# A hybrid attention and retention block: second half's retention gate, queries and keys as seven block products, h sums kept in HBM

## The chip, the core and the metric

The kernel is one program on one NeuronCore of a Trainium2 chip. The metric is the device time of one execution in microseconds; the kernel before takes 517.6 us (median of three runs, 517.25 to 517.76). PE is the matmul engine, DVE and ACT the two vector engines, POOL the general one, SP the engine that only issues transfers. [...] The profile is that of one execution.

## What is computed

One decoder block over x of 512 tokens by 1024 channels, float32. Cut to what matters:

```python
h = rms_norm(x, norm_pre)
(q_n, k_c, v_c, k_s, v_s, k_w, v_w, g_n, z_n,
 q_r, k_r, v_r, z_r, m_a, m_b) = jnp.split(h @ w_in, split_points(), axis=-1)
o_a = nsa(rope(q_n), rope(k_c), v_c, rope(k_s), v_s, rope(k_w), v_w, g_n + b)   # three masked softmaxes, gated
y_a = (o_a * silu(z_n)) @ w_nsa_o
o_b = retention(rope(q_r), rope(k_r) * 128 ** -0.5, v_r)     # 4 heads, chunks of 128, a state R per head, group norm
y_b = (o_b * silu(z_r)) @ w_ret_o
merged = sigmoid(m_a) * y_a + sigmoid(m_b) * y_b
y = x + rms_norm(merged @ w_out, norm_post)
```

w_in is 1024 by 6936. With 512 tokens every selected block is in reach and the window covers all of the past, so the selected and the sliding branch are two full causal attentions.

## The kernel before

**Number form.** Every large product takes float32 operands split in two parts of a rounded format, a high part (whi, hTh) and a low part (wlo, hTl), and uses three matmuls per tile: high by high, low by high, high by low. ACT rounds the high part (L204), DVE subtracts for the low part (`sub_split`, L216). The normed input h lies transposed in hTh and hTl, 8 tiles of 128 channels by 512 tokens; the norm's factor per token is applied to the products (`rs`).

**Weight stream.** All weights lie in HBM in the order of use. SP loads them in pieces of 512 KB into four buffers `raw` (`load_next`, L385 and L388); `splitter` and `split_lo` make whi and wlo of them, each piece in two halves, up to nine halves ahead of PE. A load waits for the low part that frees its buffer.

**Order of work.** One Python pass writes all queues: coroutines ask for buffers and times, class `Order` keeps a clock per engine with assumed costs, and issues whichever is due (`run`; `MARGINS` and `SLACK` set how late a piece counts as due). Nothing of the order is decided on the chip: each engine follows its queue, and waits where an operand is late. The blocks of PE's main line are, after the attention projections and the compression products, those of PLAN: Z (attention's gate), MA (merge gate a), ZR, QK and VR (retention gate, queries with keys, values of heads 0 and 1), ZR, QK and VR of heads 2 and 3, MB, the output products NO and RO, and the second halves MA, NO, MB, RO, last the product with w_out. Attention's steps (`att_head`, `att_block`, `att_cmp`, `att_sum`) are laid between the matmuls of Z to VR, retention's (`ret`) between those of VR and later.

**Seven products.** The second halves of MA and MB and the w_out product do a 2 by 2 block product with seven instead of eight block products (Strassen's scheme in Winograd's form). It needs sums of weight quarters and sums of h quarters. The weight sums are made in HBM: POOL issues copies and accumulating transfers (`weight_sums` L365 and L367, for MA and MB; `out_sums` L351 and L353, for w_out). Those of MA and MB are let go in portions as attention's tiles finish (`CAPS`, released by a one-element copy `mark`, L983, which holds POOL's queue until that tile is there). Those of w_out are issued three or one at a time behind retention's steps: in `ret`, POOL raises the variance to the power -0.5 (`rv`, L216) for the group norm, and `OSUMS` transfers follow. The h sums for MA and MB are made late (`h_sums`, `h_sum`): xT is loaded again, ACT scales it, DVE adds and subtracts, and both split.

**Second half of retention.** ZR and QK of heads 2 and 3 are two blocks, for each of four token tiles 8 x 3 matmuls of 512 columns (`nat`): 192 in all. `tail_zr` makes the gate, `tail_qk` rotates queries and keys straight from the accumulator.

**Attention's small products.** `tail_q` rotates a tile of queries, splits it, and transposes the rounded pair of each head (eight groups of four transposes). `att_cmp` doubles the probabilities of the compressed branch and transposes two blocks for each of two groups.

Of the kernel before, what the change touches and what calls it, by code (L numbers as in the profile page):

```python
# [28 lines left out]
PLAN = (("Z", 0), ("MA", 0), ("ZR", 0), ("QK", 0), ("VR", 0), ("ZR", 1), ("QK", 1), ("VR", 1),  # L29
# [6 lines left out]
MARGINS = {"att_sum": 400.0, "tail_m": 250.0}  # L36
SOON = 2
ISSUE = 8.0
SLACK = 900.0
WAKE = 7  # L40
HOLD_C = 1800.0
EARLY = 1300.0
HOLD = 800.0
OSUMS = (3, 3, 3, 3, 1, 1, 1, 1)
CAPS = (0, 4, 8, 11, 14, 16, 16, 16, 16)
DVE_BIAS = 400
# [97 lines left out]
def block_kernel(ctx: ExitStack, tc, x, xT, x0s, ws, small, w2s, norm_post, rope_r, dmask, out):  # L144
# [5 lines left out]
    cp.tile([P, 48], FT, name="pad")  # L150
# [108 lines left out]
    identp = ep.tile([P, P], FT, name="identp")  # L259
# [31 lines left out]
    xt = [at(o, D) for o in (16, 20, 32, 0)]  # L291
# [4 lines left out]
    KD2 = Ring([at(8 + i, 256) for i in range(2)])  # L296
    NAT = Ring([bp.tile([P, 512], FT, name=f"nat{i}") for i in range(4)])
    PR = Ring([at(8 + 2 * i, 512) for i in range(8)])
    SMC = Ring([(at(27, 256).rearrange("p (h c) -> p h c", h=8), at(24, 512).rearrange("p (h c) -> p h c", h=8))])
# [6 lines left out]
    sgw = [bp.tile([P, 2048], FT, name="sg"), at(30, 2048)]  # L306
# [3 lines left out]
    XH = Ring([at(o, 512) for o in (38, 40)])  # L310
# [12 lines left out]
    sums, osums, oissued, atts = [], [], [], [0]  # L323
    mark = sp.tile([P, 1], FT, name="mark")
    for pieces in stream_shape():
        if pieces == "seven":
            b11, b12, b21, b22 = (ws[off + i * P * 1024:off + (i + 1) * P * 1024].rearrange("(p n) -> p n", p=P)
                                  for i in range(4))
            t1, t2, t3, t4 = (dp.tile([P, 1040], FT, name=f"t{len(sums)}{i}")[:, 0:1024] for i in range(4))
            sums.append(((t1, b11), (t3, b12), (t2, b11), (t4, b21), (t1, b12), (t3, b22), (t2, t3), (t4, t2)))  # L330
# [3 lines left out]
        if pieces == "out":  # L334
            b11, b12, b21, b22 = ([ws[off + i * P * 1024:off + (i + 1) * P * 1024].rearrange("(p n) -> p n", p=P)
                                   for i in range(2 * q, 2 * q + 2)] for q in range(4))
            t1, t2, t3, t4 = ([dp.tile([P, 1040], FT, name=f"o{i}{j}")[:, 0:1024] for j in range(2)] for i in range(4))
            for a, b in ((t1, b11), (t3, b12), (t2, b11), (t4, b21), (t1, b12), (t3, b22), (t2, t3), (t4, t2)):
                osums.extend(zip(a, b))
            loads.extend((a, [1024]) for q in (b11, t3, t2, t4, t1, b21, b22) for a in q)  # L340
            continue
        loads.append((off, pieces))
        off += P * sum(pieces)

    def out_sums(n):

        for _ in range(n):
            i = len(oissued)
            o, a = osums[i]
            if i < 8:  # L350
                G.dma_start(o, a)  # L351
            else:
                G.dma_start(o, a, accum_op=OP.add)  # L353
            od.op("pool", 900.0)
            oissued.append(i)

    def weight_sums():

        for n in range(8):
            for i, block in enumerate(sums):  # L360
                while n * len(sums) + i >= CAPS[atts[0]]:
                    yield lambda: n * len(sums) + i < CAPS[atts[0]]
                o, a = block[n]
                if n < 4:
                    G.dma_start(o, a)  # L365
                else:
                    G.dma_start(o, a, accum_op=OP.add)  # L367
                od.op("pool", 900.0)
# [4 lines left out]
    def in_ring(p):  # L373

        return min(p, KD) + max(p - 2 * KD, 0)
# [20 lines left out]

    def used_up(r):

        done.append(r)
# [3 lines left out]
    def splitter():  # L403
        for i, (_, pieces) in enumerate(loads):
            n = sum(pieces)
            for k in range(2):
                p = 2 * i + k
                late = p - 2 * len(loads) + 8
                own = KD <= p < 2 * KD or late >= 0
                if late >= 0:  # L410
                    yield od.need("gb")
                yield lambda: own or in_ring(p) < in_ring(len(done)) + NW
# [4 lines left out]
                r = max(raws[i][1], done[-1] if done and not own else 0.0)  # L417
# [3 lines left out]
                if late >= 0:  # L421
                    hi, lo = at(4 * late, 512, FR), at(4 * late + 2, 512, FR)
                elif own:
# [5 lines left out]
                if p:  # L429
# [8 lines left out]
    def split_lo(p, hi, lo, src, vh, vl, r):  # L438
        yield lambda: rank(p)() == 0 or od.eng["dve"] <= od.now + SLACK
        yield r  # L440
        r = sub_split(vl, src, vh, r)
# [7 lines left out]
    def rank(p):  # L449

        return lambda: 0 if p <= wanted[0] + SOON else 4

# [50 lines left out]
    x0 = ep.tile([P, KD + 256], FT, name="x0")  # L503
# [12 lines left out]
    def load_x(t):  # L516
        r = max(hready[0:2]) if t == NT - 1 else 0.0
        DMA.dma_start(xt[t], x[t * P:(t + 1) * P, :])
        xr_[t] = od.dma(P * D * 4, r)
# [12 lines left out]
    def h_low(k, e):  # L532
# [3 lines left out]
        od.flags.add(f"h{k}")  # L536

# [87 lines left out]
    def tail_a(t, ps, e, ring):  # L625
# [12 lines left out]
        yield e + HOLD  # L638
# [35 lines left out]

    def tail_z(j, ps, e):
# [9 lines left out]
        NAT.put(th, e)  # L685
        od.flags.add(f"Z{j}")
# [95 lines left out]
    def tail_q(t, ps, e):  # L782
# [6 lines left out]
        qs = qT[t].rearrange("p h (s c) -> p h s c", s=2)  # L789
        qv = qn.rearrange("p (h c) -> p h c", h=8)  # L790
# [4 lines left out]
        for g in range(2):  # L795
            pt = yield from PT.get()
            yield e + PE_LAG
            for j in range(4):
                ep = tr(pt.bitcast(FR)[:, j * P:(j + 1) * P],
                        qs[:, g * 4 + j].rearrange("p a b -> p (a b)"), identr, e)  # L800
            yield ep, "act"
            ep = act(qT[t][:, g * 4:g * 4 + 4, :], pt.rearrange("p (h c) -> p h c", h=4), r=ep)
            PT.put(pt, ep)
# [15 lines left out]
    def att_cmp(t):  # L819
# [5 lines left out]
        for h in range(8):  # L825
# [20 lines left out]
        e = tt(s3.rearrange("p h (r c) -> p h r c", r=2), sm.unsqueeze(2).broadcast_to([P, 8, 2, 32]),  # L846
               zc.unsqueeze(2).unsqueeze(3).broadcast_to([P, 8, 2, 32]), OP.mult, e)
        for g in range(2):
# [9 lines left out]
            pv = pc.rearrange("p (i j c) -> p i j c", i=2, j=2)  # L858
            tv = pt[:, 0:2 * P].rearrange("p (i c) -> p i c", i=2)
            yield ep, "act"  # L860
            for j in range(2):
                eh = act(pv[0:64, :, j, :], tv[j * 64:j * 64 + 64], r=ep)
            yield eh, "dve"
            for j in range(2):
                ep = tt(pv[32:64, :, j, :], tv[j * 64 + 32:j * 64 + 64], f(pv[32:64, :, j, :]), OP.subtract, eh)
# [5 lines left out]
    def att_head(t, g, brs, j, slot, stat):  # L871
# [6 lines left out]
        e = mm(sv, q, kB[:, b0:b0 + nb, g, 0:L], False, True)  # L878
        yield e, "dve"
# [12 lines left out]
        slot["pv"], slot["z"] = pv, e  # L892

# [73 lines left out]
    def att_sum(t, g, po):  # L967
# [10 lines left out]
        yield e, "pool"  # L978
# [4 lines left out]
        G.tensor_copy(mark[m], gv[:, 0, 0:1])  # L983
        od.op("pool", 70.0, e)
        atts[0] += 1
# [35 lines left out]
    def tail_qk(hp, t, ps, e):  # L1021
        yield od.need("q0", "q1", "q2", "q3", "cmp0", "cmp1", *([f"ret{hp - 1}{t}"] if hp else []))
# [12 lines left out]
        ACC.put(ps, e)  # L1035
        if 4 * hp + t + 1 < 8:
            load_rtab(4 * hp + t + 1, e)
        yield e, "pool"
# [15 lines left out]
        od.flags.add(f"qk{hp}{t}")  # L1054

    rr, dmr, qend = [0.0], [], [0.0] * NT

    def ret(hp, t, ps, e):
# [24 lines left out]
        if t < NT - 1:  # L1083
            knh, knl = yield from KNHL.get()
            ek = act(knh, kf[t])
            yield ek, "pool"
# [47 lines left out]
        if hp or t >= 2:  # L1134
            VR[1].put((vh, vl), e)
        yield eo, "dve"
# [9 lines left out]
        out_sums(OSUMS[4 * hp + t])  # L1146
# [70 lines left out]
    shr = [0.0] * 4  # L1217

    def h_sums():

        yield od.need(*[f"qk1{t}" for t in range(NT)], *ATT)
        for k in range(4):
            if k == 1:
                yield od.need("ga", *RETA)
                sum_tiles()
                od.flags.add("sums")
            xs = []
            for i in range(2):
                if k:
                    xs.append((yield from XH.get()))  # L1230
                else:
                    xs.append((maskp, at(28, 512))[i])
                DMA.dma_start(xs[i], xT[(4 * i + k) * P:(4 * i + k + 1) * P, :])
                e = od.dma(P * 2048, 0.0) + 1500.0
            od.spawn(h_sum(k, xs, e), 5)

    def h_sum(k, xs, r):
        yield od.need("sums")
        yield r, "act"
        for i in range(2):  # L1240
            e = act(xs[i], xs[i], r=r, scale=gp[:, 4 * i + k:4 * i + k + 1])
        a = yield from NAT.get()
        b = yield from NAT.get()
        yield e, "dve"
        tmp = (a[:, 0:256], a[:, 256:512], b[:, 0:256], b[:, 256:512])
        a11, a21, a12, a22 = (xs[i // 2][:, i % 2 * 256:(i % 2 + 1) * 256] for i in range(4))
        e2 = tt(tmp[2], a22, a21, OP.subtract, e)
        e0 = stt(tmp[0], tmp[2], -1.0, a11, OP.mult, OP.subtract, e2)
        yield e0, "dve"
        e1 = tt(tmp[1], a11, a21, OP.subtract, e)  # L1250
# [553 lines left out]
```

## Time and profile before

| what | value |
|---|---|
| median of three runs | 517.6 us |
| the profiled execution | 517.32 us, span 515.4 us |
| granted PE clock | 0.999 |
| PE, weight loads, DVE, ACT, POOL busy | 506.2, 433.7, 419.2, 303.8, 40.1 us |
| HBM read, written | 77.79 MB, 18.87 MB |
| transfers issued by SP (q1), by POOL (q0) | 62.99 MB, 16.78 MB |

The span goes from the first instruction to the last; the execution has some 1.9 us around it. A row of a timeline gives start, duration, engine, line, operation, out<-in and count; a row of a table of stretches gives the stretch, its length, busy time (and instructions) of PE, weight loads, DVE, ACT and POOL, the granted clock, the DMA engines' mean busy share and GB/s. In a row of DMA queues stand packets, MB and the share of 16 engines' time.

### The profile page before, as it was taken

The page shows a single profiled execution, that of the slowest core. Times are in us where ns is not written, and L with a number is a line of the kernel's source. Part 1 is how long each engine was busy: PE and PEld are TensorE (multiplying, and loading weights), DVE is VectorE, ACT ScalarE, POOL GpSimd, SP SyncE. Part 2 cuts the span into 40 slices and gives each one's busy share as a digit, 9 for nine tenths or more (in the row PEclk, how much of TensorE's full clock was granted, in tenths as well). Part 3 has the DMA queues.
Part 4 walks back from the last instruction along what each step waited for, and adds up shares of the span by engine and source line. Part 5 has one row for each costly group of instructions (what it writes and reads, how often), then busy time and mean ns, then how long its engine had stood idle before and what let it go on. Part 6 is the DMA issues. An engine that isn't in the chain of part 4 may idle for free.

```text
span 515.4 us, 7802 instructions
## 1 busy us (share of the span) xinstructions
PE 506.2 (98%) x2714; PEld 433.7 (84%) x2714; DVE 419.2 (81%) x990; ACT 303.8 (59%) x659; POOL 40.1 (8%) x76
## 2 busy tenths in 40 slices
PE   9999999999999999999999999999999999999995
PEld 7898788888888888888888888888888999988884
DVE  5798799988979798887776666787997876889796
ACT  6673599677677989662544443462664434437642
POOL 3000000000211011100303100202000000000010
PEclk9999999999999999999999999999999999999999
DMA  8942026501764637634565944272842745453814
GB/s 314 373 165 83 22 82 212 197 1 41 239 210 104 184 52 171 167 95 151 169 239 128 257 117 132 42 245 42 250 159 79 229 143 162 157 174 122 318 53 160
DMA packets 25624, 80.39 MB, mean 156 GB/s; under 512 B 2801, under 2 KB 4081, under 8 KB 25585
## 3 DMA queue, kind: packets, MB, share of 16 engines
q1 hardware_dynamic: 20832, 62.99, 35.8%
q0 software_dynamic: 4608, 16.78, 14.1%
q8 instruction: 21, 0.34, 0.3%
q14 instruction: 19, 0.15, 0.1%
q10 hardware_dynamic: 144, 0.14, 0.1%
HBM read 77.79 MB, written 18.87 MB: 188 GB/s over the span
## 4 chain that ended last, share of the span: by engine, by line
PE 88%; DVE 5%; DMA 4%; ACT 1%; issue 1%; SPq 0%; DVEq 0%; POOLq 0%; POOL 0%; ACTq 0%
PE bank L237 75%; PE bank L1555 7%; PE bank L241 6%; DMA arena_l<-in_x_dram 2%; DVE arena_r L216 1%; DMA arena_l<-in_xT_dram 1%; DMA raw<-in_stream_dram 1%; DVE wlo L216 1%; DVE arena_f L216 1%; ACT arena_r L204 1%; DVE arena_l L885 0%; DVE nat L216 0%; DVE arena_l L216 0%; SPq L513 0%; SPq L385 0%
## 5 line engine op out<-in xcount | busy, mean ns | idle before, releaser
L204 ACT ACTIVATE whi<-raw 128x512 fp32r<-128x512 f32 x160 | 96.7, 627 | 44.4 <-PE bank L237 34.7
L216 DVE TENSOR_TENSOR wlo<-raw,whi 128x512 fp32r<-128x512 f32 x176 | 115.4, 684 | 8.6 <-ACT whi L204 8.0
L237 PE MATMUL bank<-whi,hTh 128*128 128x512 f32 x256 | 100.0, 406 | 0.2 <-ACT hTh L204 0.2
L237 PE MATMUL bank<-whi,hTl 128*128 128x512 f32 x256 | 96.2, 391 | 0.0
L237 PE MATMUL bank<-wlo,hTh 128*128 128x512 f32 x256 | 96.1, 391 | 0.0
L237 PE MATMUL bank<-arena_r 128*128 128x256 f32 (+2 forms) x328 | 69.5, 335 | 0.0
L237 PE MATMUL bank<-arena_r,whi 128*128 128x512 f32 (+1 forms) x208 | 63.6, 381 | 0.0
L216 DVE TENSOR_TENSOR arena_r<-bank,arena_r 128x512 fp32r<-128x512 f32 (+2 forms) x80 | 48.1, 606 | 18.1 <-ACT arena_r L204 17.5
L204 ACT ACTIVATE arena_r<-bank 128x512 fp32r<-128x512 f32 (+2 forms) x88 | 46.6, 536 | 23.8 <-PE bank L241 21.0
L204 ACT ACTIVATE arena_l<-arena_l,stat 128x384 f32<-128x384 f32 (+3 forms) x102 | 54.0, 557 | 7.4 <-DVE stat L885 4.0
L237 PEld LDWEIGHTS bank<-whi,hTl 128*128 128x128 f32 x256 | 48.0, 188 | 10.6
L237 PEld LDWEIGHTS bank<-whi,hTh 128*128 128x128 f32 x256 | 48.6, 190 | 9.0 <-ACT hTh L204 0.5
L237 PEld LDWEIGHTS bank<-arena_r 128*128 128x128 f32 x328 | 50.8, 190 | 5.7
L237 PEld LDWEIGHTS bank<-wlo,hTh 128*128 128x128 f32 x256 | 48.2, 188 | 8.4
L237 PE MATMUL bank<-hTh,whi 128*128 128x512 f32 (+1 forms) x144 | 52.6, 365 | 0.0
L237 PE MATMUL bank<-hTh,wlo 128*128 128x512 f32 (+1 forms) x144 | 51.2, 355 | 0.0
L237 PE MATMUL bank<-hTl,whi 128*128 128x512 f32 (+1 forms) x144 | 51.1, 355 | 0.0
L237 PEld LDWEIGHTS bank<-arena_r,whi 128*128 128x128 f32 x208 | 39.0, 188 | 7.4
L237 PE MATMUL bank<-arena_r,wlo 128*128 128x512 f32 x96 | 37.4, 389 | 0.0
L241 PE MATMUL bank<-ident,arena_l 128*128 128x128 f32 x216 | 32.3, 272 | 0.0
L241 PEld LDWEIGHTS bank<-ident,arena_l 128*128 128x128 f32 x216 | 26.8, 140 | 6.5
L237 PEld LDWEIGHTS bank<-hTh,wlo 128*128 128x128 f32 x144 | 27.2, 189 | 4.0
(211 smaller groups left out, 817.1 us busy)
## 6 DMA issues: line engine op xcount, KB each, us to landing
raw<-in_stream_dram SPq DMA_DIRECT2D x75, 512.0 KB, 4.3
t<-in_stream_dram POOLq DMA_DIRECT2D x12, 512.0 KB, 5.1
o<-in_stream_dram POOLq DMA_DIRECT2D x12, 512.0 KB, 5.3
raw<-t SPq DMA_DIRECT2D x8, 512.0 KB, 3.4
raw<-o SPq DMA_DIRECT2D x8, 512.0 KB, 3.9
arena_f<-in_rope_r_dram SPq DMA_DIRECT2D x8, 256.0 KB, 2.7
t<-t POOLq DMA_DIRECT2D x4, 512.0 KB, 5.9
o<-o POOLq DMA_DIRECT2D x4, 512.0 KB, 5.3
```

The lines of the kernel that those rows point to most:

```text
L204: S.activation(o, i, func, **kw)
L216: (V if e == "dve" else G).tensor_tensor(o, a, b, op=op)
L237: T.matmul(ps, a, b, start=start, stop=stop)
L241: T.transpose(ps, a, idn)
L1555: T.matmul(ps[m], a, b, start=n in first and s + i == 0, stop=n in last and s + i == 5, skip_group_check=True)
```

## The change

Four parts.

1. **PAIR.** The blocks ZR 1 and QK 1 become one block `pair`: the 512 tokens by 1024 columns (queries, keys, gate) over 1024 channels as seven products of 24 matmuls. A product goes into two accumulator banks, X and Q in turn, and a bank is used again when its content was kept (ACT copies it to `Z` or `U`) or joined (DVE adds the kept part). The gate and the rotation then read from SBUF.
2. **h sums in HBM.** Early, ACT scales xT by plus or minus the norm's weight (`signed`), SP stores the quarters (22 stores of 128 KB), and POOL adds three tables in HBM (`hsums`). The sums are then loaded in the weight stream, once for PAIR and once for MA and MB, and split like weights into `SB`. `h_sums` and `h_sum` go.
3. **All sums at once.** `add_sums(27)` issues every copy and accumulation in one row behind one `mark`, which waits for the first tile of Z: PAIR's, the h sums, MA's and MB's together in transfers of 1 MB, then w_out's. `OSUMS` is zero. The room for descriptors of POOL's transfers is four times as large.
4. **Smaller ones.** `tail_q` transposes first (four groups of four) and splits after, `att_cmp` transposes one block per group, the loads and order constants are set anew.

```diff
-PLAN = (("Z", 0), ("MA", 0), ("ZR", 0), ("QK", 0), ("VR", 0), ("ZR", 1), ("QK", 1), ("VR", 1),
+PLAN = (("Z", 0), ("MA", 0), ("ZR", 0), ("QK", 0), ("VR", 0), ("PAIR", 1), ("VR", 1),
...
-OSUMS = (3, 3, 3, 3, 1, 1, 1, 1)
-CAPS = (0, 4, 8, 11, 14, 16, 16, 16, 16)
-DVE_BIAS = 400
+OSUMS = (0, 0, 0, 0, 0, 0, 0, 0)
+FIRST = 27
+DVE_BIAS = 500
...
+    hsums = [(two(s02), s21.unsqueeze(1).broadcast_to([P, 2, 1024])), (s1, stab[0]), (s3, s1)]
...
+    sums = ((t1, b11), (t3, b12), (t2, b11), (t4, b21), (t1, b12), (t3, b22), (t2, t3), (t4, t2))
+    seq = [(o, a, i >= 4) for s in (psums, sums, osums) for i, (o, a) in enumerate(s)]
+    for i, h in zip((4, 7, 9), hsums):
+        seq[i:i] = [(*h, True)]
...
+    def add_sums(n):
...
+            o, a, add = seq[issued[0]]
+            if add:
+                G.dma_start(o, a, accum_op=OP.add)
             else:
                 G.dma_start(o, a)
+            od.op("pool", 7000.0 if add else 1000.0)
...
     def weight_sums():
...
+        yield od.need("hq", "Z0")
+        G.tensor_copy(mark, szn[:, 0, 0:1])
+        od.op("pool", 70.0, zready[0])
+        add_sums(FIRST)
...
+    def signed(k, e):
...
+        for i in range(2):
+            e = act(o[i], v[i], r=e, scale=(gp, ngp)[(i + k // 4 + 1) % 2][:, k:k + 1])
+        yield e + 200.0
+        c = slice(k % 4 * 256, k % 4 * 256 + 256)
+        for t, i in ((stab[2], 1), (stab[1], 1), (s21, 0)) if k < 4 else ((stab[0], 0), (stab[3], 1)):
+            DMA.dma_start(t[:, c], o[i])
...
-        e = act(qs[:, :, 0, :], qv, r=e)
-        yield e, "dve"
-        e = sub_split(qs[:, :, 1, :], qv, qs[:, :, 0, :], e)
+        pt = yield from PT.get()
+        yield e + PE_LAG
+        for i in range(4):
+            ep = tr(pt[:, i * P:(i + 1) * P], qn[:, i * P:(i + 1) * P], ident, e)
...
-            for i in range(2):
-                ep = tr(pt[:, i * P:(i + 1) * P],
-                        s3[:, g * 4 + 2 * i:g * 4 + 2 * i + 2, :].rearrange("p h c -> p (h c)"), ident, e)
+            ep = tr(pt[:, 0:P], s3[:, g * 4:g * 4 + 4, :].rearrange("p h c -> p (h c)"), ident, e)
...
+    def pair():
+        blk = Block(36, 512)
+        X, Q = [(yield from ACC.get())], []
+        U, Z = (maskp, at(22, 512)), zt[1]
...
+        plan = ((X, quarter(0, 0), None), (Q, summed(2), 4), (X, summed(1), 10), (Q, quarter(1, 1), None),
+                (X, summed(0), 20), (Q, quarter(0, 1), None), (X, summed(3), 30))
...
+            if n >= 2:
+                lst = {2: p1, 3: p7, 4: u1}.get(n)
+                if lst is not None:
+                    yield lambda: len(lst) == 2
+                    r = max(lst)
+                else:
+                    yield lambda: all((n - 2, m) in fr for m in range(2))
+                    r = max(fr[n - 2, m] for m in range(2))
+                yield r + PE_LAG
...
+                        for j, (a, b) in enumerate(((lh, wh), (ll, wh), (lh, wl))):
+                            T.matmul(ps[m], a, b, start=n in first and s + j == 0, stop=n in last and s + j == 5,
+                                     skip_group_check=True)
...
-    nc = bacc.Bacc("TRN2", target_bir_lowering=False, num_devices=1, dynamic_dma_scratch_size=512)
+    nc = bacc.Bacc("TRN2", target_bir_lowering=False, num_devices=1, dynamic_dma_scratch_size=2048)
```

How the order moves, at two places. POOL's queue from the last sums of MA and MB to retention's first groups, before (t are the sums of MA and MB, o those of w_out, L351 copies and L353 and L367 add):

```order
L367 DMA t_119<-t_117 128x1024
L367 DMA t_123<-t_121 128x1024
L983 COPY mark<-arena_l 64x1 x3
L216 TENSOR_TENSOR rv<-rv,nhalf 128x2
L351 DMA o_124<-in_stream_dram 128x1024
L351 DMA o_125<-in_stream_dram 128x1024
L351 DMA o_128<-in_stream_dram 128x1024
L216 TENSOR_TENSOR rv<-rv,nhalf 128x2
```

The same place now (out are the sums of w_out, L376 copies and L374 adds):

```order
L376 DMA out_126<-in_stream_dram 128x2x1024
L376 DMA out_128<-in_stream_dram 128x2x1024
L376 DMA out_127<-in_stream_dram 128x2x1024
L376 DMA out_129<-in_stream_dram 128x2x1024
L374 DMA out_126<-in_stream_dram 128x2x1024
L374 DMA out_128<-in_stream_dram 128x2x1024
L374 DMA out_127<-out_128 128x2048
L374 DMA out_129<-out_127 128x2048
L216 TENSOR_TENSOR rv<-rv,nhalf 128x2 x8
```

All sums stand ahead of the first of the eight rv, where w_out's stood between them. DVE's queue in the second half, before, where retention's gate and rotation follow each other (wlo are low parts of weights, L229 on nat rotates from the accumulator):

```order
L216 TENSOR_TENSOR wlo<-raw,whi 128x512 x4
L216 TENSOR_TENSOR arena_r<-bank_91,arena_r 128x4x128
L216 TENSOR_TENSOR wlo<-raw,whi 128x512 x3
L229 SCALAR_TENSOR_TENSOR arena_l<-nat_113,arena_l 128x512
L229 SCALAR_TENSOR_TENSOR nat_111<-bank_87,rs_135,arena_f 128x4x64 x2
L229 SCALAR_TENSOR_TENSOR nat_110<-bank_87,rs_135,arena_f 128x4x64 x2
L216 TENSOR_TENSOR nat_111<-nat_111,nat_110 128x4x64 x2
```

And now, in PAIR (maskp<-bank and arena_l<-bank of 512 columns are joins, arena_r<-raw low parts of h sums):

```order
L216 TENSOR_TENSOR maskp<-bank_93,maskp 128x512
L216 TENSOR_TENSOR arena_l<-bank_92,arena_l 128x512
L216 TENSOR_TENSOR wlo<-raw,whi 128x512 x2
L216 TENSOR_TENSOR arena_r<-raw,arena_r 128x512
L216 TENSOR_TENSOR arena_r<-arena_l,arena_r 128x256
L216 TENSOR_TENSOR arena_r<-raw,arena_r 128x512
L216 TENSOR_TENSOR arena_l<-bank_86,arena_l 128x512
L216 TENSOR_TENSOR arena_l<-bank_87,arena_l 128x512
L229 SCALAR_TENSOR_TENSOR nat_111<-maskp,rs_133,arena_f 128x4x64 x2
```

Joins and low parts of h sums stand between the low parts of weights, and the rotation reads the joined tile maskp instead of a bank.

More of the change, by code (lines that the diff above doesn't have):

```diff
@@ L328, in block_kernel @@
                                   for i in range(4))
-            t1, t2, t3, t4 = (dp.tile([P, 1040], FT, name=f"t{len(sums)}{i}")[:, 0:1024] for i in range(4))
-            sums.append(((t1, b11), (t3, b12), (t2, b11), (t4, b21), (t1, b12), (t3, b22), (t2, t3), (t4, t2)))
+            t1, t2, t3, t4 = (t[:, len(svoff) * 1024:(len(svoff) + 1) * 1024] for t in tsv)
+            if not svoff:
+                for w in (11, 12, 10, 13):
+                    sload[len(loads)] = w
+                    loads.append((stab[w - 10], [1024]))
+            svoff.append(off)
             loads.extend((a, [1024]) for a in (b11, b21, t2, t3, t1, t4, b22))
@@ L333, in block_kernel @@
             continue
[L334 to L340, printed above, removed]
+        if pieces in ("pair", "out"):
+            b11, b12, b21, b22 = (ws[off + 2 * q * P * 1024:off + (2 * q + 2) * P * 1024]
+                                  .rearrange("(j p n) -> p j n", j=2, p=P) for q in range(4))
+            t1, t2, t3, t4 = (two(dp.tile([P, 2064], FT, name=f"{pieces}{i}")[:, 0:2048]) for i in range(4))
+            (osums if pieces == "out" else psums).extend(
+                ((t1, b11), (t3, b12), (t2, b11), (t4, b21), (t1, b12), (t3, b22), (t2, t3), (t4, t2)))
+            for n, q in enumerate((b11, t3, t2, t4, t1, b21, b22)):
+                if pieces == "pair" and n in (1, 2, 4, 6):
+                    sload[len(loads)] = w = {1: 2, 2: 1, 4: 0, 6: 3}[n]
+                    loads.append((stab[w], [1024]))
+                loads.extend((q[:, j, :], [1024]) for j in range(2))
+            off += 8 * P * 1024
             continue
@@ L373, in in_ring @@
     def in_ring(p):
-        return min(p, KD) + max(p - 2 * KD, 0)
+        return min(p, KD) + max(p - 2 * KD, 0) - sum(min(max(p - 2 * i, 0), 2) for i in sload)
     hook = {}
@@ L416, in splitter @@
                         load_next()
-                r = max(raws[i][1], done[-1] if done and not own else 0.0)
+                r = max(raws[i][1], done[-1] if done and not own else sfree.get(sload.get(i), 0.0))
                 yield r, "act"
@@ L449, in rank @@
     def rank(p):
-        return lambda: 0 if p <= wanted[0] + SOON else 4
+        return lambda: 0 if p <= wanted[0] + (PSOON if p in pairp else SOON) else 4
+    pairp = range(2 * min(sload) - 4, 2 * sorted(sload)[3] + 6)
     class Block:
@@ L673, in tail_c @@
         od.flags.add(f"C{t}")
+    zready = [0.0]
     def tail_z(j, ps, e):
@@ L1270, in product @@
             if wait:
-                yield od.need(*[f"sh{k}" for k in range(2 * p, 2 * p + 2)])
-                yield max(shr[2 * p:2 * p + 2]) + PE_LAG
+                yield sblk[0].ready(wait - 2 + p)
+                yield sblk[0].ready(wait - 2 + p)
             yield blk.ready(2 * n + p)
@@ L1286, in seven @@
     def seven(name, half):
+        if not sblk:
+            sblk.append(Block(8, 512))
+            for _ in range(8):
+                used_up(done[-1])
         blk = Block(14, 512)
@@ L1310, in seven_end @@
         yield od.need(*[f"mg{k}" for k in range(4)])
-        if not st["off"]:
-            yield od.need("sh3")
         if n == 3:
@@ L1659, in main @@
                 yield from seven(name, i)
+                continue
+            if name == "PAIR":
+                yield from pair()
                 continue
@@ L1768, in stream @@
         out += block(name, i)
-    out += [a for r in range(2) for c in range(2) for a in pair(w_out[r * 512:(r + 1) * 512, c * 512:(c + 1) * 512])]
+    out += quarters(w_out)
     return np.concatenate([o.reshape(-1) for o in out])
```

315 lines of the change are left out of this document (199 added, 116 removed).

## The prediction

> **What bounds the kernel now.** I read the page's busy times first, then its chain of waits, then the PE timeline, and last the stretches on which the change leans.
>
> ```profile
> PE 506.2 (98%) x2714; PEld 433.7 (84%) x2714; DVE 419.2 (81%) x990; ACT 303.8 (59%) x659; POOL 40.1 (8%) x76
> PE 88%; DVE 5%; DMA 4%; ACT 1%; issue 1%; SPq 0%; DVEq 0%; POOLq 0%; POOL 0%; ACTq 0%
> ```
>
> The busy share alone would not prove it, since a pipelined matmul's end is modelled. What proves it is the chain (88% on PE) and the distance from one matmul's start to the next. From the chain's pieces in order of time and from the PE timeline:
>
> ```profile
> 471.23 35.37 PE bank L1555 x156
> 198.97 0.60 PE L241 MATMUL bank<-ident,arena_l 128*128 128x128 f32 x4
> 199.32 0.48 PE L237 MATMUL bank<-whi,hTh 128*128 128x512 f32 x1
> 199.63 0.40 PE L237 MATMUL bank<-wlo,hTh 128*128 128x512 f32 x1
> 199.87 0.40 PE L237 MATMUL bank<-whi,hTl 128*128 128x512 f32 x1
> ```
>
> The 156 matmuls of the output product take 35.37/156 = 0.227 us each, and in the middle of the program, at 199.63 to 199.87, the distance is the same 0.24 us. The only longer step there is the first matmul after a group of transposes (199.32 to 199.63, 0.31). So PE goes at its own pace through nearly the whole span, and an instruction taken from it is worth its pace, as long as nothing new is late. [...]
>
> **What comes off PE.** Retention gate, queries and keys of the second half are 96 + 96 matmuls of 128x512 now. Seven products of 24 are 168: 24 x 0.227 = 5.4 us less. Two smaller edits also touch PE:
>
> ```profile
> 79.51 0.54 PE L241 MATMUL bank<-identr,arena_r 128*128 128x128 f32 x4
> 79.89 1.16 PE L237 MATMUL bank<-arena_r 128*128 128x512 f32 x4
> 81.80 0.46 PE L241 MATMUL bank<-identr,arena_r 128*128 128x128 f32 x4
> 82.09 0.46 PE L237 MATMUL bank<-arena_r 128*128 128x512 f32 x1
> 113.72 0.38 PE L241 MATMUL bank<-ident,arena_l 128*128 128x128 f32 x2
> 113.86 0.47 PE L237 MATMUL bank<-hTh,whi 128*128 128x512 f32 x1
> ```
>
> The attention queries were transposed as rounded pairs, eight groups of four that hold PE 0.38 and 0.29 us, 0.34 in the mean: 2.7 us. Now four groups of plain float32, each 0.35 plus 0.08 for the step after it (198.97 to 199.63): 1.7 us. That is 1.0 less. The compressed branch transposes one block where it had two, eight times. Four transposes take 0.35, so each of these 0.09: 0.7 less. **Sum on PE: 5.4 + 1.0 + 0.7 = 7.1 us.**
>
> **The sums in HBM, the new wait.** All 27 transfers that add weight quarters and h quarters now stand on POOL behind one mark (it waits for the first tile of Z's gate), and ahead of every rv (the power that gives retention's group norm its 1/sigma). rv therefore waits until the last of them can be issued, and that one needs the end of the one before it. Behind rv on DVE stand the normalisation, then the weight splits; PE's transposes wait for the first and its weights for the second. So the question is when the sums end against when rv is due. Rows: the mark's release, the first rv, the pace of the present sums, the DMA queues from 101 to 245 us, and three stretches.
>
> ```profile
> 101.14 0.68 DVE L229 SCALAR_TENSOR_TENSOR arena_l<-nat,arena_l 128x512 f32<-128x512 f32 x1
> 245.51 0.73 POOL L216 TENSOR_TENSOR rv<-rv,nhalf 128x2 f32<-128x2 f32 x1 [10.39 <-DVE rv L223]
> 190.71 0.81 POOL L367 DMA_DIRECT2D t<-t  x1 [4.61 <-issue]
> 196.27 0.83 POOL L367 DMA_DIRECT2D t<-t  x1 [4.75 <-issue]
> q0 software_dynamic: 2304, 8.39, 25.3%
> q1 hardware_dynamic: 3408, 9.70, 20.6%
> 136.00:154.00 18.00, 18.00 (x103) 15.47 (x102) 14.40 (x39) 13.26 (x32) 4.58 (x10) 1.00 0.70 237
> 191.50:196.00 4.50, 4.50 (x26) 3.75 (x25) 4.36 (x20) 4.13 (x13) 0.02 (x1) 1.00 0.71 117
> 101.00:245.00 144.00, 144.00 (x756) 121.31 (x755) 123.75 (x338) 103.88 (x258) 13.56 (x24) 1.00 0.46 127
> ```
>
> Time at hand: 245.5 - 101.8 = 143.7 us; the new order has as much PE work between the two points (0.7 of transposes less, three matmuls more). Work: eight copies of 512 KB are alone in 136 to 154 (DMA 0.70 x 18 = 12.6 us), 1.6 each; q0 as a whole holds 25.3% of 144 = 36.4, so the eight accumulations take (36.4 - 12.6)/8 = 3.0 each (one alone, 191.5 to 196: 0.71 x 4.5 = 3.2). Ahead of rv's release now stand 12 copies of 1 MB (37.8), and 12 accumulations of 1 MB with two of 512 KB (26 x 3.0 = 78). SP's own loads stay 20.6% of 144 = 29.7. **Together 145.5 us of full DMA work for 143.7 us.** On top come the times in which the queue is empty because one accumulation needs the end of another: 190.71 to 196.27 is 5.56 us for 3.0 us of data, so 2.6 each. There are five such places ahead of rv; in two of them the short h sums fill the queue, so 3 x 2.6 = 7.8 us, which SP's 29.7 us of loads can use as well. So rv is late by 1.8 us if the loads fill every hole, and by 9.6 if none. POOL has been held to one accumulation at a time (4.6 us of "issue" before each, though its operands were long there); the change gives the descriptors four times the room for transfers twice as large, so I take two or more in flight. In the order 15 matmuls stand between rv and the transposes that need it, 3.4 us, of which rv 0.73 and three DVE steps use about 2.5: one us of slack. Cost to PE: 0.8 to 8.6 us, and nothing if accumulations run a little faster in a full queue. I take 1, near the lower end, because the loads are nearly four times the holes.
>
> [...]
>
> **DVE in the second half.** The stretch from the second gate's start to the end of the second values is 260 to 338 us:
>
> ```profile
> 260.00:338.00 78.00, 78.00 (x396) 65.89 (x395) 54.31 (x120) 33.92 (x65) 9.26 (x12) 1.00 0.54 147
> 60.00:100.00 40.00, 38.68 (x237) 33.31 (x237) 37.18 (x92) 34.61 (x77) 0.00 (x0) 1.00 0.47 159
> 364.57 1.89 DVE L216 TENSOR_TENSOR wlo<-raw,whi 128x512 fp32r<-128x512 f32 x3
> PEld bank L237 <- DVE wlo L216: 1.4, 1, 1.4
> ```
>
> In the new order 143 DVE instructions stand there for 120: 14 more low parts of weights, 6 low parts of h sums, 6 joins of a product with a kept one, 3 others fewer. Back to back such a step takes 1.89/3 = 0.63, so 23 x 0.63 = 14.5 us: DVE 69 of the 72.5 us that remain to PE. The nearest row is 60 to 100 us, where DVE is busy 37.2 of 40 and PE loses 1.3, mostly one wait for a weight's low part (1.4). Bounds: nothing, or 72.5/40 x 1.3 = 2.4. I take 1. The same row prices the queries' new low parts: eight half-height steps for four full ones, 4 x 0.63 = 2.5 us more DVE in a place that has 2.8 idle. Bounds 0 and 2.5; I take 0.3, since 2.8 us of idle time can hold nearly all of it.
>
> **Edits that I cost at nothing.** Sixteen scalings of xT on ACT and 22 stores of 128 KB on SP, between the norm and the query block. Cover: ACT is busy 8 of 20 us there and the DMAs 0.21.
>
> ```profile
> 40.00:60.00 20.00, 20.00 (x107) 16.68 (x105) 16.30 (x51) 8.21 (x19) 0.23 (x1) 1.00 0.21 66
> 365.00:400.00 35.00, 35.00 (x164) 29.26 (x163) 31.01 (x66) 20.55 (x43) 0.00 (x0) 1.00 0.49 167
> ```
>
> The stores stand ahead of weight loads on SP's queue and wait for ACT; were the scalings late, the loads for the compression weights would be late next, at most by the 1.4 us that PE waits there already. In return the h sums' own arithmetic leaves DVE and ACT after 365 us. PE does not wait there (35.00 of 35), so nothing is gained. The four h-sum loads for the merge gates and the eight stay-put loads replaced balance on SP. Start and end of the program keep their steps.
>
> **Sum.** 7.1 - 1 - 1 - 0.3 = 4.8 us off the span: 515.4 to 510.6. The profiled execution took 517.3, 1.9 more than its span and 0.3 less than the median of the runs: 517.3 - 4.8 = **512.5 us** (512.8 on the median's scale). Its own bounds are all costs at zero with the 1.4 us wait for a weight gone too, 517.3 - 7.1 - 1.4 = 508.8, and the two DVE costs at their upper ends, 517.3 - 7.1 + 1 + 2.4 + 2.5 = 516.1.
>
> **Rivals.** *The sums come last (slower).* One mechanism: POOL reaches the first rv only when the DMA work ahead is done, and everything behind it on DVE stands. If no hole is filled rv is 9.6 us late and the accumulations of one alone (3.2 for 3.0) add 26 x 0.2 = 5.2, so 13.8 beyond the slack: 517.3 - 7.1 + 13.8 + 1.3 = 525.3; with the holes alone, 520.1. If POOL is still held to one accumulation at a time, each costs 3.0 + 5.56 = 8.6 for a full MB: 37.8 + 12 x 8.6 + 2 x 5.6 = 152, and the loads beside it half hidden 15: 23 us late, some 534. It is slower from a stall of 7.1 - 1.3 + 1 = 6.8 us on. For it: 145.5 against 143.7 is no margin. Against it: accumulations in a full queue have no holes. Chance 0.17, most of it near 520. *DVE takes PE's place (no change).* The pair's products, joins, rotations and gate tails fight for DVE, which has 3.5 us left of 72.5, each product needs the join two products back, and what PE saved it waits away: with waits of 5 us in place of 1.3, and the sums' 1, 517.3 - 7.1 + 6 = 516.2, and a little more gives no change. For it: 95% busy. Against it: 365 to 400 us runs at 89% with PE unbroken. Chance 0.13. *The change does more than I count*: the wait for the weight's low part goes and no sum is late, 508.8; chance 0.2. Forecast as such: 0.5.
>
> **How the numbers follow.** A difference under 0.2%, about 1 us, cannot be told from no change with these runs. Faster: 0.5 + 0.2 and 0.03 of the second rival. Same: 0.10 of it and a few of the forecast's own upper end, together 0.11, which leaves faster at 0.72. Slower: 0.17. The range goes from 508.5 to 520.5, so that it takes in the all-gain case and the sums rival at its nearer price; above it lies about a tenth.
>
> **What would show it.** The group at the pair's line has 168 matmuls at 0.227, PE's span to its last matmul some 4 to 7 us shorter, and DVE's wait "rv L216 <- POOL" short. The sums rival shows as an rv on POOL whose idle time before it ends on a DMA, with PE idle at 243 to 260; the DVE rival as PE waits for wlo, bank joins or sums between 255 and 330. Wrong altogether would be a PE pace other than 0.227 in the new products, or the first mark well after 102 us.

## Result and the profile after

The changed kernel takes 525.5 us (median of six runs, 522.8 to 527.7), the kernel before 517.8 (median of six, 517.3 to 519.0): a ratio of 1.014, 95% interval 1.011 to 1.018. It is slower, by 1.4%. The prediction was 512.5 with a range up to 520.5, so it is wrong in sign, and the time lies outside its range. The profiled execution took 524.3 us, its span 522.5.

Of the page of the kernel after, the busy times and the chain of waits by engine:

```profile
PE 505.5 (97%) x2666; PEld 430.5 (82%) x2666; DVE 433.0 (83%) x1010; ACT 317.4 (61%) x700; POOL 40.2 (8%) x65
PE 82%; DVE 8%; DMA 6%; issue 1%; ACT 1%; DVEq 0%; POOLq 0%; POOL 0%; SPq 0%; ACTq 0%
```

From the chain's pieces of the same kernel (start, duration, what), the last 156 matmuls:

```profile
477.88 35.37 PE bank L1696 x156
```

The chain has 6 points less on PE, 3 more on DVE and 2 more on DMA. The output product keeps its 35.37 us but starts at 477.88, where it started at 471.23 before.

**Where the time went.** I took the distance between the starts of two consecutive matmuls, and what it exceeds the median distance of that shape by, summed per stretch. The medians summed are PE's work, the excess is what PE lost. How finely shapes are told apart moves the work and the losses somewhat, but the extra loss between 200 and 260 us stays near 10. Worked out from the traces, in us (the third column is the kernel without any sums, below; the last the fastest one found that gives the whole result):

```
stretch            before   after   without sums   copies early
work (medians)      494.2   487.3       487.1          487.1
  0 to  40            2.6     4.0         3.2            3.1
 40 to 100            4.2     4.6         5.0            4.9
100 to 200            3.4     3.1         3.1            2.9
200 to 260            1.5    11.6         1.5            3.2
260 to 300            0.6     0.6         0.5            0.5
300 to 330            0.7     2.5         3.0            2.8
330 to the end        0.6     0.9         0.6            0.6
lost, sum            13.7    27.2        16.8           18.0
```

The saving is there (6.9 us of work) and 13.5 us are lost for it, 10.1 of them between 200 and 260 us. That is the first half's queries and keys, which the change does not touch. The same in the table of stretches (length, then busy time of PE, weight loads, DVE, ACT and POOL, granted clock, DMA share, GB/s), before:

```profile
205.00:260.00 55.00, 55.00 (x282) 46.36 (x281) 44.17 (x102) 30.51 (x71) 6.70 (x12) 1.00 0.51 155
295.00:330.00 35.00, 35.00 (x175) 29.27 (x174) 22.89 (x51) 14.01 (x27) 2.38 (x3) 1.00 0.43 114
```

And after:

```profile
205.00:260.00 55.00, 48.94 (x230) 39.22 (x230) 38.90 (x109) 27.68 (x81) 4.72 (x5) 0.94 0.81 229
295.00:330.00 35.00, 33.68 (x168) 27.88 (x167) 33.42 (x72) 20.59 (x40) 1.70 (x2) 1.00 0.52 165
```

PE stands idle for 6.1 of the 55 us, and its granted clock is 0.94 in the mean. The chain of waits in that stretch names what ended last: a start, a duration and what it was. After:

```profile
210.88 7.74 DMA arena_f<-in_rope_r_dram
...
221.72 7.66 DMA arena_f<-in_rope_r_dram
...
233.93 7.17 DMA raw<-in_stream_dram
...
245.54 7.15 DMA arena_l<-in_dmask_dram
```

These are four loads of SP: the rotation tables of tiles 1 and 2 (`rtab`, 256 KB, one buffer, so each is issued when the tile before has been rotated), a weight, and retention's mask. The tables' issues, before and after, give the times from issue to landing:

```profile
DMA to landing us min/median/max: 2.6/2.7/3.5
```

```profile
DMA to landing us min/median/max: 2.6/3.3/7.7
```

Each table has 256 KB. One by one, the tables of tiles 1, 2 and 3 take 3.3, 2.6 and 3.5 us before, and 7.7, 7.7 and 2.8 after: two of the three are late. While the rotation waits DVE runs nothing else (5.07 us at the second table), and PE's transposes need what comes behind it. DVE's timeline at the second table (in brackets the idle time before and what ended it), after:

```profile
229.47 0.88 DVE L229 SCALAR_TENSOR_TENSOR nat<-bank,rs,arena_f 128x256 f32<-128x256 f32 x2 [5.07 <-DMA arena_f<-in_rope_r_dram]
```

From the waits of the kernel after, in us, times, longest:

```profile
DVE nat L229 <- DMA arena_f<-in_rope_r_dram: 7.9, 2, 5.1
...
PE bank L241 <- DVE nat L216: 4.1, 2, 3.3
```

By the distances between matmuls, PE loses 1.6 us at 219.2 us (behind the first table), 3.5 at 229.6 (behind the second), 2.7 to a half clock right after that, and 1.5 at 252.0 (behind the mask): 9.3 of the 10.1. The late weight on the chain stopped PE nowhere by itself.

What the first table met is in the DMA queues during its flight, 210.9 to 218.6 us (packets, MB, share of 16 engines), after:

```profile
q0 software_dynamic: 596, 2.29, 88.4%
q1 hardware_dynamic: 183, 0.36, 13.6%
out<-in_stream_dram POOLq DMA_DIRECT2D x2, 1024.0 KB, 16.3
arena_f<-in_rope_r_dram SPq DMA_DIRECT2D x1, 256.0 KB, 7.7
```

In flight were w_out's last three copies (they landed at 214.2, 217.4 and 220.3 us) and its first two accumulations (issued at 210.0 and 214.6). The table's 128 packets of 2 KB took 0.1 us each, 8 per DMA engine in the mean; in the same time 35 packets of the sums per engine were done (560 of 4 KB). SP's queue got 13.6% of the engines' time, about a seventh. Before, in the flight of the second table, q1 is alone:

```profile
q1 hardware_dynamic: 144, 0.26, 33.0%
```

### The profile page after: what moved, and what is told of

The parts are those of the page before. It is cut to its first block, busy times and chain, and to the rows that moved or that the text cites. A ratio compares the mean times of both kernels' runs of the same rounds, so it can differ in the third digit from the quotient of the medians.

```text
span 522.5 us, 7837 instructions
## 1 busy us (share of the span) xinstructions
PE 505.5 (97%) x2666; PEld 430.5 (82%) x2666; DVE 433.0 (83%) x1010; ACT 317.4 (61%) x700; POOL 40.2 (8%) x65
## 4 chain that ended last, share of the span: by engine, by line
PE 82%; DVE 8%; DMA 6%; issue 1%; ACT 1%; DVEq 0%; POOLq 0%; POOL 0%; SPq 0%; ACTq 0%
PE bank L237 64%; PE bank L1206 7%; PE bank L1696 7%; PE bank L241 5%; DMA arena_f<-in_rope_r_dram 3%; DVE wlo L216 2%; DVE arena_r L216 2%; DVE nat L229 1%; DMA raw<-in_stream_dram 1%; DMA arena_l<-in_dmask_dram 1%; DMA sg<-in_x_dram 1%; DVE nat L216 1%; DVE arena_l L939 1%; ACT whi L204 0%; DVE arena_l L223 0%
## 5 line engine op out<-in xcount | busy, mean ns | idle before, releaser
L237 PE MATMUL bank<-whi,hTh 128*128 128x512 f32 x192 | 75.1, 412 | 1.2 <-ACT hTh L204 0.6
L237 PE MATMUL bank<-whi,hTl 128*128 128x512 f32 x192 | 72.8, 400 | 0.0
L237 PE MATMUL bank<-wlo,hTh 128*128 128x512 f32 x192 | 72.7, 400 | 0.0
L204 ACT ACTIVATE arena_r<-bank 128x512 fp32r<-128x512 f32 (+3 forms) x104 | 49.1, 476 | 32.5 <-PE bank L241 29.3
L216 DVE TENSOR_TENSOR arena_r<-bank,arena_r 128x512 fp32r<-128x512 f32 (+3 forms) x104 | 55.7, 542 | 10.1 <-ACT arena_r L204 8.9
L204 ACT ACTIVATE arena_l<-arena_l,stat 128x128 f32<-128x128 f32 (+3 forms) x104 | 53.5, 542 | 12.1 <-DVE stat L216 9.2
L237 PEld LDWEIGHTS bank<-whi,hTh 128*128 128x128 f32 x192 | 37.3, 195 | 9.2 <-ACT arena_l L204 1.0
L237 PEld LDWEIGHTS bank<-whi,hTl 128*128 128x128 f32 x192 | 37.0, 193 | 8.2
L237 PEld LDWEIGHTS bank<-wlo,hTh 128*128 128x128 f32 x192 | 37.2, 194 | 7.2 <-DVE wlo L216 0.3
L939 DVE CUSTOM_DVE_ANT_0 arena_l<-bank,maskp 128x512 f32<-128x512 f32 (+3 forms) x64 | 29.4, 484 | 2.9 <-PE bank L237 2.6
```

The costliest lines, as they stand in the source:

```text
L204: S.activation(o, i, func, **kw)
L216: (V if e == "dve" else G).tensor_tensor(o, a, b, op=op)
L237: T.matmul(ps, a, b, start=start, stop=stop)
L939: V.tensor_tensor_reduce(pv[:, b, :], sv[:, b, :], maskp[:, 512 - L:512], 1.0, -NEG, OP.add, OP.min, nm[:, b:b + 1])
```

## Experiments

Three theories were put to the runs. *Tables*: just-in-time loads, the tables first, land late beside the sums of w_out. *Order*: the new order of DVE's work is late there by itself. *Traffic*: the sums slow all loads, also those issued early. Each ratio is against runs of the kernel before on the same chip. Each diff shows the lines that matter.

**Without any sums.** In place of the 27 transfers nothing; the loads take plain weight blocks, so the sums are left out of the result.

```diff
...
-            loads.extend((a, [1024]) for a in (b11, b21, t2, t3, t1, t4, b22))
+            loads.extend((a, [1024]) for a in (b11, b21, b12, b21, b12, b22, b22))
...
-            if add:
-                G.dma_start(o, a, accum_op=OP.add)
-            else:
-                G.dma_start(o, a)
```

> The changed kernel without any of the 27 sums in HBM: the loads take plain weight blocks in their place (the sums of weights and of h are left out of the result). Everything else stays. Tables theory: a little under the one without w_out's early sums, 512-516. Traffic theory: clearly less than with the tables left out, 510-513. Order theory: 522-526, since what is late is not a transfer. The prediction's own sum without any loss to the sums is 517.3 - 7.1 + 1.3 = 511.5.

Measured: 513.2 us, ratio 0.992 (0.989 to 0.994). Its two stretches:

```profile
205.00:260.00 55.00, 55.00 (x287) 46.52 (x286) 47.56 (x128) 35.27 (x96) 1.42 (x2) 1.00 0.30 90
295.00:330.00 35.00, 33.47 (x170) 27.61 (x169) 32.10 (x68) 18.91 (x38) 1.67 (x2) 1.00 0.34 110
```

And its output product, from the chain's pieces:

```profile
467.26 35.38 PE bank L1692 x156
```

PE is unbroken from 205 to 260 us, so the order theory falls: the same order without sums loses nothing there. The sums cost 525.5 - 513.2 = 12.3 us (11.8 by the two ratios to the kernel before). The 1.5 us at 295 to 330 stay without sums, so they belong to the rest of the change: there DVE is busy 32.1 of 35 us, where it was 22.9 before.

**One table.** Tiles 1 to 3 are rotated with the table of tile 0; the sums stay.

```diff
-        DMA.dma_start(rtab, rope_r[i // 4, i % 4 * P:(i % 4 + 1) * P, :])
+        if i not in (1, 2, 3):
+            DMA.dma_start(rtab, rope_r[i // 4, i % 4 * P:(i % 4 + 1) * P, :])
```

> The changed kernel, but the rotation tables of tiles 1 to 3 of the first half's queries and keys are not loaded: these tiles are rotated with the table of tile 0 (that part of the result is left out). Nothing else moves on any engine. Tables theory (after the change a table lands some 7.2 us after its issue, beside the sums of w_out, in place of 2.7, and each tile's rotation waits for it, VectorE with it and TensorE behind): without the loads TensorE's losses between 205 and 255 us (11 us over its pace) shrink to 2 or 3, and the time falls from 525.5 to 515-518. Order theory (the new order of VectorE's work is what is late there, tables or not): 524-526. Traffic theory (the sums slow all loads, those of weights as well): 521-525, since the weights are as late as before.

Measured: 516.0 us, ratio 0.996 (0.994 to 0.997), as the tables theory said. Three loads of 256 KB are worth 9.5 of the 12.3 us, though every sum still runs. (With the loads, SP's wait for the table's buffer goes too; this run does not tell the two apart. The executions of both kernels scatter over 4 to 5 us, and the two profiled spans differ by 7.1.) What is left there is the next load that has no time to spare, retention's mask, again beside an accumulation. Its piece of the chain:

```profile
235.68 8.77 DMA arena_l<-in_dmask_dram
```

And PE's timeline at its end:

```profile
245.53 1.68 PE L237 MATMUL bank<-arena_r 128*128 128x256 f32 x6 [2.33 <-ACT arena_r L204]
```

The traffic theory falls in its plain form: the loads of weights at 100 to 200 us, issued early enough, run beside 19 sums and PE loses no more than before (3.1 us for 3.4 in the table above).

**Late tables without sums.** The kernel before, with each of the three tables loaded three times in a row.

```diff
-        DMA.dma_start(rtab, rope_r[i // 4, i % 4 * P:(i % 4 + 1) * P, :])
+        for _ in range(3 if i in (1, 2, 3) else 1):
+            DMA.dma_start(rtab, rope_r[i // 4, i % 4 * P:(i % 4 + 1) * P, :])
```

> The kernel before, with each of the tables of tiles 1 to 3 of the first half's queries and keys loaded three times in a row into its place (the same data; each load waits for the one ahead of it). No sum is moved. A table is then ready some 7 to 8 us after its first issue, as after the change, in place of 2.7. Tables theory: the distance of the tiles' rotations grows from 6.7 us to 9-11, TensorE stands at 215 to 245 us, and the time rises by 4 to 11 us, to 522-529; where TensorE stands for over 2 us the granted clock falls behind it. Rival (late tables are covered by other work on VectorE and TensorE, and it was the sums in the data path that hurt): 518-519.5.

Measured: 529.6 us, ratio 1.022 (1.020 to 1.024), just above the range of the tables theory. The chain at the last of the three tables:

```profile
235.71 3.31 DMA arena_f<-in_rope_r_dram
239.04 2.70 DMA arena_f<-in_rope_r_dram
241.75 2.65 DMA arena_f<-in_rope_r_dram
```

The timelines of DVE and of PE behind it:

```profile
244.49 0.88 DVE L229 SCALAR_TENSOR_TENSOR nat<-bank,rs,arena_f 128x256 f32<-128x256 f32 x2 [3.69 <-DMA arena_f<-in_rope_r_dram]
...
246.86 0.50 PE L237 MATMUL bank<-wlo,hTh 128*128 128x512 f32 x1 [3.21 <-DVE wlo L216]
```

And the stretch that follows:

```profile
248.00:252.00 4.00, 3.75 (x11) 3.03 (x12) 2.22 (x5) 1.49 (x3) 0.00 (x0) 0.57 0.60 214
```

Tables that take some 8 us cost about 12 us in the old kernel with no sum moved (in part since SP stands meanwhile too, with a weight's load behind it). DVE waits 11.5 us for the three tables here, and 7.9 for two in the kernel after. So the wait of the kernel after is shown from both sides: take the late loads away and most of the loss goes, make them late by other means and it comes.

**w_out's sums early in the kernel before.** 12 of its 16 sums ahead of the first half's queries and keys.

```diff
+        for i, (o, a) in enumerate(osums[:12]):
+            if i < 8:
+                G.dma_start(o, a)
+            else:
+                G.dma_start(o, a, accum_op=OP.add)
...
```

> The kernel before, with 12 of the 16 sums of w_out (eight copies and four accumulations of 512 KB) issued right behind the sums of the merge gates, so at some 196 us, ahead of the first half's queries and keys, and not behind retention's first four steps. Tables theory: the tables of tiles 1 to 3 land in 5 to 7 us in place of 2.7, and the time rises by 3 to 9 us, to 521-527. Order theory: no change, 517-518. Traffic theory: 519-523.

Measured: 527.2 us, ratio 1.016 (1.011 to 1.020). The size is at the upper end of the tables theory, and the tables did land late, in 5.3, 6.5 and 5.5 us, with one idle time of PE of 2.0 us right behind the second. But the longest one, 5.0 us, has another reason, so the size must not be counted for the theory. The timelines of POOL, DVE and PE:

```profile
253.71 0.82 POOL L373 DMA_DIRECT2D o<-in_stream_dram  x1 [4.71 <-issue]
...
255.31 0.73 POOL L216 TENSOR_TENSOR rv<-rv,nhalf 128x2 f32<-128x2 f32 x1
...
256.07 0.99 DVE L225 TENSOR_SCALAR arena_l<-bank,mv,rv 128x256 f32<-128x256 f32 x2 [6.64 <-POOL rv L216]
...
258.98 1.11 PE L241 MATMUL bank<-ident,arena_l 128*128 128x128 f32 x4 [4.98 <-DVE arena_l L216]
```

POOL issues one accumulation at a time here, 5 to 9 us apart, and rv stands behind them: this is the mechanism of the prediction's slower rival, in the kernel before. That the small room for descriptors holds it back was not shown; the larger room was not tried by itself.

**Other places for w_out's eight sums.** All keep the other engines' order.

```diff
-FIRST = 27
+FIRST = 19
-OSUMS = (0, 0, 0, 0, 0, 0, 0, 0)
+OSUMS = (1, 1, 1, 1, 1, 1, 1, 1)
...
```

> The changed kernel, but only 19 sums stand behind the first mark; the eight sums of w_out follow one by one behind the eight retention steps, as in the kernel before. The other engines' order is the same. Tables theory: from some 200 us on no sum runs beside the tables, they land in about 3 us, and the time is 513-517. Traffic theory: the same or less, 512-516. Order theory: 524-526. If the new sums behind retention's steps hold rv back in turn, TensorE stalls at 255 to 345 and the time stays over 520.

Measured: 516.5 us, ratio 0.998 (0.996 to 0.999), as the tables theory said. PE is unbroken from 205 to 260 us (55.00 of 55.00 busy); at 295 to 330 it loses 2.8 us (32.24 of 35.00 busy), and its granted clock is 0.95 there. On the chain there stands no late transfer but ACT, whose copy of a bank is behind a split that waits for PE. Why that is longer here than without sums stays open.

The copies behind retention's first two steps, the accumulations behind its last (`FIRST = 19`, `OSUMS = (2, 2, 0, 0, 0, 0, 0, 4)`):

> The changed kernel with 19 sums behind the first mark; of w_out's eight, the copies follow two by two behind retention's first two steps (some 245 and 255 us) and the four accumulations behind its last one (some 330 us), so that no sum runs beside a table of the first half nor of the second (300 to 320 us). Tables theory: the losses at 300 to 312 us that were left with the sums one by one (5.1 us over the pace) come down to the 2.5 of the kernel without any sums, and the time to 513-515, 0.6 to 0.9% under the kernel before. If those losses are the order of the seven products itself, and not the sums beside it: 516-517. If accumulations beside the later weight loads cost as much: 517-520.

Measured: 517.7 us, ratio 1.000 (0.998 to 1.001). All eight behind the last step (`FIRST = 19`, `OSUMS = (0, 0, 0, 0, 0, 0, 0, 8)`):

> The changed kernel with 19 sums behind the first mark and all eight of w_out behind retention's last step (from some 330 us on). Tables theory: neither the first half's tables nor the second half's meet a sum, nor do the loads of the seven products (where the copies beside them cost 5 us at 270 us), so TensorE's losses are those of the kernel without any sums, and the time is 513-514.5, 0.7 to 0.9% under the kernel before. If the eight together are late for the output product's loads or slow the weights from 340 us on: 515-520.

Measured: 521.1 us, ratio 1.005 (1.004 to 1.007). The tables theory missed both times: the tables of the first half landed in time, but the sums met other loads. The first kernel came out where its third reading had put it (517 to 520), and the second is outside both of its ranges. The longest transfers on the chain, of the first kernel near 270 us and of the second at 375 to 410:

```profile
258.75 10.29 DMA raw<-pair
```

```profile
374.44 9.40 DMA raw<-s
...
395.82 8.97 DMA raw<-t
```

Weights and h sums that land in 4.1 to 4.7 us in the kernel after (medians) took 9 to 10 here, and nothing ahead of them covered that.

The copies stay early, the four accumulations go behind the last step (`FIRST = 23`, `OSUMS = (0, 0, 0, 0, 0, 0, 0, 4)`):

> The changed kernel with 23 sums behind the first mark: w_out's four copies of 1 MB stay there (some 196 to 210 us), its four accumulations go behind retention's last step. If the accumulations alone are what the tables meet (they ran at 210 to 250 us): 513-516, as with the copies moved too. If the copies reach into the first table's load (211 us on) : 516-520, with the first table late and the others not.

Measured: 514.7 us, ratio 0.995 (0.993 to 0.997): **faster than both kernels**, by half a percent against the one before. The time is that of the first forecast, the way that of the second: only the first table is late, beside the end of the copies, and it costs less than expected. Its piece of the chain, and the stretch:

```profile
210.00 7.87 DMA arena_f<-in_rope_r_dram
```

```profile
205.00:260.00 55.00, 53.48 (x278) 45.07 (x277) 45.66 (x126) 33.79 (x93) 1.43 (x2) 1.00 0.43 149
```

Last, the same with the copies ahead of MA's and MB's last two accumulations, to fill a hole in the data path:

```diff
+    seq[17:23] = seq[19:23] + seq[17:19]
...
```

> As with the four accumulations of w_out behind retention's last step and its copies early, but the copies stand ahead of the last two accumulations of MA and MB, for which POOL had waited (20 and 8 us), so that they fill the 6 us of empty data path at 180 to 195 us. Tables theory: the first table, issued at 210 us, then lands in 3 to 6 us and not in 7.5, TensorE's stall of 1.7 us at 218 us goes or shrinks, and the time is 513-514.5 against 514.7. If the copies only push the last two accumulations into the table's load: 514.5-517.

Measured: 520.2 us, ratio 1.004 (1.003 to 1.006), a miss. The hole (in the kernel with the copies early a DMA share of 0.53 at 180 to 185 us and 0.37 at 190 to 195) had been what a weight needed; with the data path full from 160 to 205 us (a share of 0.93 or more in every 5 us) its load takes 12 us, ACT waits 6.03 us for it, and PE loses some 6.5 us between 200 and 210 (4.86 of the 10 us busy, with a granted clock of 0.68 in the second half). The piece of the chain and ACT's timeline:

```profile
192.87 12.12 DMA raw<-in_stream_dram
```

```profile
205.02 0.63 ACT L204 ACTIVATE whi<-raw 128x512 fp32r<-128x512 f32 x1 [6.03 <-DMA raw<-in_stream_dram]
```

## Why the prediction was wrong

**PE's saving: right.** 7.1 us predicted, 6.9 measured as work. The seven products run at PE's pace; their four pieces on the chain hold 116 matmuls in 26.5 us, 0.229 each:

```profile
269.69 4.76 PE bank L1206 x21
275.29 7.59 PE bank L1206 x33
285.04 8.19 PE bank L1206 x36
294.08 5.99 PE bank L1206 x26
```

**DVE in the second half: right mechanism, undersized.** I took 1 us with 2.4 as the upper bound; without any sums PE loses 1.5 of 35 us there, and by the distances 3.0 for 0.7, so 2.3. For the queries' new low parts I took 0.3; 40 to 100 us costs 0.8 more without sums and 0.4 more after, and no run tells what of it is theirs. The start, where I took no change, costs 0.5 to 1.4 more from 0 to 40 us, and no run was made for its cause. The stores of signed xT are 20 in the trace, where I wrote 22. Together the kernel without sums came to 513.2, where the prediction's terms give 511.5.

**The sums: the wrong wait.** The prediction asked whether the 27 sums end before rv, and put the cost of that at 1 us. That wait cost nothing. POOL around the last sum and the first rv, after:

```profile
240.68 0.81 POOL L374 DMA_DIRECT2D out<-out  x1 [8.01 <-DMA out<-out]
256.48 0.73 POOL L216 TENSOR_TENSOR rv<-rv,nhalf 128x2 f32<-128x2 f32 x1 [15.00 <-DVE rv L223]
```

Two accumulations ran at once, as I had taken it (issued at 210.0 and 214.6 us, landed 15.8 and 16.9 us later). The last was issued at 240.7 us, ahead of the 245.5 at which rv was due before, where I had worked out a delay of 1.8 to 9.6; and POOL stood for 15 us before rv, for DVE and not for a transfer.

The step that failed is the one that counted SP's 29.7 us of loads as work that fills holes in the DMA's time, and put the cost of their landing late at nothing, without a reason. I added up capacity (145.5 us of work in 143.7), but PE waited on the latency of single loads: with the data path as full as I had just worked out, two tables took 7.7 us each, and they had no slack for that. The runs put 12.3 us on the sums where I had 1, and 9.5 of them go with the three table loads.

The rows that would have told were in the trace of before: three tables issued one after the other at 214.5, 220.9 and 227.8 us, and used 1.2, 1.9 and 1.5 us after their landing. A table that takes 7.7 us uses up its slack and keeps DVE waiting for some 3 us, 9 us for three. That this meets the 9.5 us of the run with one table is partly luck: in the profile two tables were late, with DVE waits of 2.9 and 5.1 us, and the clock's fall and the late mask did the rest.

**The slower rival** gave 520 to 534 at 0.17 by way of rv. The size came true by luck, for the way did not: rv was late by 11 us (245.5 before, 256.5 after) because what DVE has ahead of it was late. That its own way is real shows in the kernel before with early sums (DVE waits 6.64 us for rv there). **DVE takes PE's place** did not happen beyond the term above. That fewer matmuls do shorten the way shows in the kernel without sums: PE's last product starts 4.0 us earlier there (467.26 for 471.23).

## What to carry to other kernels

Adding up DMA work against the time at hand told here whether the background transfers end in time (the last was issued at 240.7 us, with rv due at 245.5 before); it did not tell what they do to the loads beside them (7.7 us for a table that took 2.6 to 3.5 before). List the loads that are issued just in time (one buffer, issued at release), take their slack from the trace, and keep bulk transfers out of those stretches, or give these loads a second buffer (which was not tried here). Each move of a bulk transfer wants that list anew: of five places for the same eight sums, one gave 0.5%, one 0.2%, and three gave nothing or cost time.

## What the hardware showed beyond that

**A load beside sums first waited, then shared.** The first table was issued at 210.9 us, and its first packet moved 3.7 us later; before, the second table's moved after 1.0 us. The DMA queues from 212.0 to 214.5 us, after:

```profile
q0 software_dynamic: 213, 0.83, 93.2%
q1 hardware_dynamic: 2, 0.00, 0.0%
```

Then, from 214.5 to 217.8 us, the table's 128 packets moved among those of the sums:

```profile
q0 software_dynamic: 223, 0.86, 78.0%
q1 hardware_dynamic: 142, 0.26, 24.4%
```

That took 3.2 us in place of 1.2, and 0.8 in place of 0.4 went by from the last packet to the landing. The second table's parts are the same within 0.1 us. So over half of the delay passed before a packet of the table moved. From 212.0 to 214.5 us some 13 packets of the sums per engine moved (213 in all); the order on one engine is not in these rows, and what the table waited for stays open.

**PE's clock fell behind some idle times.** After PE's idle time of 3.33 us up to 233.4 us, matmuls of 512 columns start 0.43 us apart in place of 0.23 (PE's timeline after):

```profile
229.64 0.39 PE L237 MATMUL bank<-whi,hTl 128*128 128x512 f32 x1
233.36 1.12 PE L241 MATMUL bank<-ident,nat 128*128 128x128 f32 x4 [3.33 <-DVE nat L216]
...
235.55 0.63 PE L237 MATMUL bank<-wlo,hTh 128*128 128x512 f32 x1
235.98 0.63 PE L237 MATMUL bank<-whi,hTl 128*128 128x512 f32 x1
```

The granted clock is 0.50 from 233.4 to 239.0 us. Eight such steps cost 8 x 0.2 = 1.6 us on top of the idle time, and the transposes and the first matmul ahead of them 1.1 more. An idle time of 2.33 us (one table) also had it, with a granted clock of 0.74 at 244 to 248 us and 0.83 at 248 to 252; so had one of 4.98 us (w_out's sums early in the kernel before, 0.50 at 260 to 264) and one of 2.05 us (w_out's sums one by one, 0.71 at 304 to 308). One of 1.52 us (copies early) had not, nor one of 2.02 us (w_out's sums early in the kernel before): the clock stayed at 1.00 behind both. Nor did it always fall at once: behind 3.21 us (late tables without sums) the next three matmuls still started 0.34 and 0.23 us apart, and only behind a further 0.42 us of idle time were they 0.43 apart (a clock of 1.00 at 244 to 248 us, 0.57 at 248 to 252). What else decides it stays open; this was not tried by itself. The kernel's time varied along with it: the granted clock of the six runs after lies between 0.984 (the slowest) and 0.995, that of the kernel before between 0.996 and 0.999.
